# A fused encoder layer on one core: the first sequence's normed operand built from its loaded transposed x, with the row scales spread by four transposes

## The chip, the cores and the metric

One Trainium2 chip, and one of its cores. A core has a matrix engine (PE, with its weight loads shown as PEld), a vector engine (DVE), a scalar engine (ACT), a general engine (POOL) and a queue that issues transfers (SP). The metric is the device time of one execution in microseconds (us), as the median of several runs.

## What is computed

Two sequences of 512 tokens by 1024 features go through the same encoder layer. Cut to what this change bears on:

```python
h = rms_norm(x, ln1)             # x * rsqrt(mean(x*x) + EPS) * ln1, per token
proj = h @ w_in                  # q, k, v, u, g_att, g_ssm
...                              # windowed attention on q, k, v
...                              # state-space branch on u: a recurrence in time, both ways
x = x + mixed @ w_out
h2 = rms_norm(x, ln2)
return x + square(relu(h2 @ w_up)) @ w_down
```

Every product is made in three passes: each float32 operand is cut into a high part (rounded to float32r) and a low part (what the rounding left), and high by high, high by low and low by high are added up. So every operand of a product costs a copy on ACT (high) and a subtraction on DVE or POOL (low).

## The kernel before, in words

Almost all matmuls are 128x128 weights by 512 columns. The normed x stands transposed on chip, as eight blocks k of 128 features by 512 tokens for each sequence, with a high and a low tile: hT[0] for the first sequence (act_104 and act_105 in the order of instructions below), hT[1] for the second (act_106 and act_107).

**The front (lines 351 to 518).** The keys and values of the first sequence are made straight from x_t, its x as the host lays it out already transposed: eight strips k (xr of x_t, wr of the weights) are loaded; split_strip (327) makes high and low of xr times the gain of ln1, in hT[1]'s tiles, and of wr; strip_products (337) adds 12 matmuls for each strip into four banks, the heads. Since the tokens' scales are missing in it, scaled_heads (345) multiplies them in when ACT reads the four banks. Three of these banks are the same three that all later products take in turn (acc, line 81), so the first later product waits until ACT has read the first head.

The normed operand of both sequences is made another way: x is loaded by rows (xs, 128 tokens by 1024 features), square_rows (300) makes each token's mean square on ACT and its power -0.5 on POOL, scale_rows (308) multiplies the rows on DVE, and turn_rows (311) transposes one block k of four row tiles on PE (four transposes), from whose bank ACT takes the high part with the gain and DVE the low part.

**The columns.** Next come 24 columns of the projection (u, g_att, g_ssm), each with 24 matmuls for each sequence (products, 182, line 187 in the profile). They are a generator, and pull(n) emits as many of them as n units are worth, two units a matmul. They fill PE wherever the stage at hand leaves it free. The weights of column i+1 are cut into high and low (split, 169: line 177 on ACT, 178 on DVE) at the fourth and tenth matmul of column i, so where a pull stands decides where these lie on ACT and DVE. Total work is fixed: what is pulled early is missing later. some(n), in the same way, emits n small DVE instructions of the 73 that make the recurrence's coefficients.

**After the front.** pull(140); then the tables (557): 16 rounds, in each of which DVE and ACT prepare a piece (bm, transposed by PE at 610), PE multiplies it (641), and ACT writes the inputs h of the recurrence (646, 647), with pulls between; then 12 small transfers (665 to 667) and pull(28). Then the recurrence (714 to 720): 62 steps of four DVE instructions, each fed by the one before, with pull(15) or pull(14) in each. Then state_rows(0) and (1) (723, on ACT and DVE), pull(90) (738), and 32 rounds q (740) in which PE multiplies the states (750, 753) and pulls an even share of what is left of the columns.

In all these stages each engine's instructions stand in a hand-written order: an instruction that waits holds up all that stand behind it on its engine. (DVE, ACT and SP are ordered by the scheduler in the tables.) SP issues the loads in the order written: strips, rows, and the first column's weights.

## Time and profile before

| | |
|---|---|
| median of 3 runs | 1444.52 us (1444.01 to 1444.83) |
| the profiled execution | 1445.04 us |
| its span | 1443.3 us |
| PE, share of the span | 99% |
| DVE, ACT, POOL | 76%, 53%, 17% |

The profile is of one execution. Each row of its timeline gives a start and a duration in us from the start of the span, the engine, the line, the instruction, and in brackets how long the engine sat idle before it and what ended that. Rows of like instructions may be merged (x3). Instructions of one engine overlap in it: the next may start before the last has landed, so the distance from start to start (the pitch) is what an engine spends, and start plus duration is when others may use the result. A view of waits adds up who waited for whom; the chain is the path followed back from the last instruction.

### The profile page before, as it was taken

To read this page: it belongs to the slowest core of one execution; us is meant where nothing else is said; L and a number is where in the kernel's file an instruction comes from. 1 tells how busy PE (TensorE), PEld (TensorE's weight loads), DVE (VectorE), ACT (ScalarE), POOL (GpSimd) and SP (SyncE) were. 2 spreads that over 40 slices of the span, in tenths; PEclk is the share of its full clock that TensorE was granted. 3 is DMA by queue.
4 is the path that set the end of the run, shared out by engine and by line. 5 is a ranking of instruction groups with operands and counts; after the bars stand their busy time and mean duration, and the time that the engine had idled before them with its cause. 6 is when DMAs were issued, how large, how long until landed. Compare 5 with 4: busy or idle time off the path is not lost.

```text
span 1443.3 us, 22044 instructions
## 1 busy us (share of the span) xinstructions
PE 1435.6 (99%) x7997; PEld 1228.0 (85%) x7997; DVE 1094.9 (76%) x1978; ACT 762.3 (53%) x1359; POOL 244.1 (17%) x396
## 2 busy tenths in 40 slices
PE   9999999999999999999999999999999999999998
PEld 8888888889999999988888888888888888888887
DVE  7999959995458999988976588777776597575644
ACT  7678861224448887894444255455454443333332
POOL 3144443004244432263100000000000000000000
PEclk9999999999999999999999999999999999999999
DMA  7356549529651533345552344444442983464341
GB/s 297 97 170 189 168 147 327 206 91 314 227 180 59 162 107 100 119 140 189 194 190 91 129 136 173 161 160 155 151 143 96 363 319 102 146 201 145 121 131 59
DMA packets 102204, 240.23 MB, mean 166 GB/s; under 512 B 12330, under 2 KB 25130, under 8 KB 102096
## 3 DMA queue, kind: packets, MB, share of 16 engines
q1 hardware_dynamic: 62304, 139.94, 29.9%
q0 software_dynamic: 16320, 48.28, 10.2%
q10 hardware_dynamic: 23472, 50.61, 9.5%
q8 instruction: 63, 1.03, 0.3%
q14 instruction: 45, 0.37, 0.1%
HBM read 169.02 MB, written 81.82 MB: 174 GB/s over the span
## 4 chain that ended last, share of the span: by engine, by line
PE 84%; DVE 8%; issue 4%; DMA 2%; ACT 1%; POOL 1%; DVEq 0%; SPq 0%; ACTq 0%; POOLq 0%
PE bank L118 14%; PE bank L120 14%; PE bank L119 14%; PE acc L187 9%; PE acc L125 6%; PE acc L919 5%; PE po L1002 2%; PE sps L970 2%; PE sps L641 2%; PE tps L986 2%; PE sps L753 2%; PE acc L120 2%; PE acc L119 2%; PE acc L118 2%; DVE t L716 2%
## 5 line engine op out<-in xcount | busy, mean ns | idle before, releaser
L187 PE MATMUL acc<-act,c_hi 128*128 128x512 f32 x768 | 243.7, 395 | 0.0
L119 PE MATMUL bank<-b_lo,a_hi 128*128 128x512 f32 (+1 forms) x449 | 174.4, 389 | 0.0
L120 PE MATMUL bank<-b_hi,a_lo 128*128 128x512 f32 (+1 forms) x449 | 174.4, 389 | 0.0
L118 PE MATMUL bank<-b_hi,a_hi 128*128 128x512 f32 (+1 forms) x449 | 174.4, 389 | 0.0
L187 PEld LDWEIGHTS acc<-act,c_hi 128*128 128x128 f32 x768 | 142.3, 188 | 27.8 <-ACT act L316 0.9
L1714 ACT CAST a_hi<-d_a 128x1024 fp32r<-128x1024 f32 x56 | 59.1, 1055 | 177.4 <-PE bank L119 173.2
L187 PE MATMUL acc<-act,c_lo 128*128 128x512 f32 x384 | 151.3, 394 | 0.0
L1715 DVE TENSOR_TENSOR a_lo<-d_a,a_hi 128x1024 fp32r<-128x1024 f32 x56 | 68.5, 1223 | 98.5 <-ACT a_hi L1714 98.5
L118 PE MATMUL bank<-act,act 128*128 128x512 f32 x368 | 143.2, 389 | 0.0
L119 PE MATMUL bank<-act,act 128*128 128x512 f32 x368 | 143.2, 389 | 0.0
L120 PE MATMUL bank<-act,act 128*128 128x512 f32 x368 | 143.2, 389 | 0.0
L919 PE MATMUL acc<-w_hi,act 128*128 128x256 f32 x512 | 114.0, 291 | 0.1
L119 PEld LDWEIGHTS bank<-b_lo,a_hi 128*128 128x128 f32 x449 | 84.3, 188 | 17.5
L120 PEld LDWEIGHTS bank<-b_hi,a_lo 128*128 128x128 f32 x449 | 84.3, 188 | 17.5
L118 PEld LDWEIGHTS bank<-b_hi,a_hi 128*128 128x128 f32 x449 | 84.3, 188 | 17.3
L919 PEld LDWEIGHTS acc<-w_hi,act 128*128 128x128 f32 x512 | 87.0, 189 | 4.0 <-PE sps L970 0.3
L187 PEld LDWEIGHTS acc<-act,c_lo 128*128 128x128 f32 x384 | 72.2, 188 | 14.7 <-DVE c_lo L178 0.8
L125 PE MATMUL acc<-act,gc_hi 128*128 128x512 f32 x256 | 81.2, 394 | 0.3 <-POOL act L1066 0.3
L118 PEld LDWEIGHTS bank<-act,act 128*128 128x128 f32 x368 | 69.1, 188 | 14.4
L120 PEld LDWEIGHTS bank<-act,act 128*128 128x128 f32 x368 | 69.1, 188 | 14.3
L119 PEld LDWEIGHTS bank<-act,act 128*128 128x128 f32 x368 | 69.1, 188 | 14.2
L980 ACT ACTIVATE p<-p,nmx 128x257 f32<-128x257 f32 (+1 forms) x128 | 72.0, 563 | 16.5 <-DVE nmx L974 15.5
(365 smaller groups left out, 3424.4 us busy)
## 6 DMA issues: line engine op xcount, KB each, us to landing
d_a<-a_scr SPq DMA_DIRECT2D x56, 512.0 KB, 3.6
raws<-in_w_up_dram SPq DMA_DIRECT2D x32, 512.0 KB, 4.0
a_scr<-t ACTq DMA_DIRECT2D x64, 256.0 KB, 3.0
k<-in_w_down_dram SPq DMA_DIRECT2D x32, 512.0 KB, 5.6
c_raw<-in_w_ug_dram SPq DMA_DIRECT2D x48, 256.0 KB, 4.1
ct_scr<-ctab POOLq DMA_DIRECT2D x16, 512.0 KB, 4.8
ctab_in<-ct_scr POOLq DMA_DIRECT2D x16, 512.0 KB, 6.4
a_scr<-a ACTq DMA_DIRECT2D x32, 256.0 KB, 2.0
```

The costliest lines, as they stand in the source:

```text
L118: PE.matmul(ps, a[0], b[0], start=first, stop=False)
L119: PE.matmul(ps, a[0], b[1], start=False, stop=False)
L120: PE.matmul(ps, a[1], b[0], start=False, stop=last)
L125: PE.matmul(ps, w[wi][:, k, :], rows[yi], start=k + p == 0, stop=k == KT - 1 and p == 2)
L187: PE.matmul(ps, w[wi][:, k, :], hT[s][hi][:, k, :], start=n == 0, stop=n == 3 * KT - 1)
L641: PE.matmul(ps[:, i * P:(i + 1) * P], bm[:, ri, g, :], u_sb[:, gp * SH + g, :], start=True, stop=True)
L716: V.tensor_mul(t1, h[:, i], a8r)
L753: PE.matmul(o, ctab[:, g0 % SI + g, ri, 0:T * CH], st[:, ri, g].rearrange("p s k -> p (s k)"), start=False, stop=ri == 1)
L919: PE.matmul(self.ps, hT[sq][act][:, k, col:col + P], w[:, k % 4, :], start=i == 0, stop=i == 3 * KT - 1)
L980: S.activation(p, p, AF.Exp, bias=self.nmx[:, h:h + 1], scale=-1.0, accum_out=self.sums[:, h, self.qb:self.qb + 1])
L1714: S.copy(hi, src)
L1715: V.tensor_sub(lo, src, hi.bitcast(F32))
```

## The change

What it does, in the order of the diff below:

- Row tiles have five buffers in place of eight. The tiles of x_t's strips (xr) have eight, so that all stay; the heads' copies get their own tile kv.
- square_rows, for the first four row tiles, has POOL spread each token's scale over 128 columns (wide).
- spread_scales: four transposes on PE turn that into a bank in which the scales of all 512 tokens stand in every partition. It is placed between strips 4 and 5, in the bank of the warm-up matmuls (idle).
- normed_strip(k): DVE multiplies strip k in place by the gain and by that bank; ACT copies the high part to hT[0]. strip_low(k): DVE (even k) or POOL (odd k) subtracts the low part. They stand among strips 5 to 7 and after.
- The first sequence's scale_rows (four) and turn_rows (eight, with 32 transposes) go.
- The second sequence's squares and scales come after all this, and more columns are pulled ahead of its turn_rows: 24 + 66 units in place of 12 + 54. Since some() has taken fewer coefficients by then (59 of 73 in place of 64), the loop `while some(4): pull(6)` runs four times in place of three. Later pulls are 142 in place of 140, and 64 in place of 90 after the recurrence.

```diff
@@ -287,14 +287,13 @@
         lam_sb = sc.tile([P, 3, GROUPS], F32, name="lam_sb")
         pr, pi = [sc.tile([P, 9, GROUPS], F32, name=n) for n in ("pr", "pi")]
         factors = sc.tile([P, NT], F32, name="factors")
-        xs, scales, turned = [], {}, {}
-        for t in range(NT):
-            xs.append(xin.tile([P, D], F32, tag="xt", name="xt", bufs=NT))
+        xs, scales = [], {}
         rel_sb = xin.tile([N_BUCKETS + 1, N_HEADS], F32, name="rel_sb")
         oh_sb = xin.tile([N_BUCKETS + 1, LINE], F32, name="oh_sb")
         ln_sb = xin.tile([N_HEADS, LINE], F32, name="ln_sb")
 
         def load_rows(t):
+            xs.append(xin.tile([P, D], F32, tag="xt", name="xt", bufs=5))
             SP.dma_start(xs[t], x[t * P:(t + 1) * P, :])
 
         def square_rows(t):
@@ -304,6 +303,10 @@
             scales[t] = factors[:, t:t + 1]
             GP.tensor_scalar_add(ss, ss, EPS)
             GP.tensor_tensor(scales[t], ss, neg_half[:, 0:1], op=ALU.pow)
+            if t < NB:
+                if not t:
+                    spread.append(xin.tile([P, NB, P], F32, name="wide"))
+                GP.tensor_copy(spread[0][:, t], scales[t].to_broadcast([P, P]))
 
         def scale_rows(t):
             V.tensor_scalar_mul(xs[t], xs[t], scales[t])
@@ -317,10 +320,11 @@
             V.scalar_tensor_tensor(hT[s][1][:, k, :], ps, gain_1[:, k:k + 1], h.bitcast(F32),
                                    op0=ALU.mult, op1=ALU.subtract)
 
-        strips, heads = {}, []
+        strips, heads, spread, raws_t = {}, [], [], []
 
         def load_strip(k):
-            strips[k] = [xin.tile([P, HALF], F32, tag=tag, name=tag, bufs=6) for tag in ("xr", "wr")]
+            strips[k] = [xin.tile([P, HALF], F32, tag=tag, name=tag, bufs=n) for tag, n in (("xr", KT), ("wr", 6))]
+            raws_t.append(strips[k][0])
             for tile_, src in zip(strips[k], (x_t, w_kv)):
                 SP.dma_start(tile_, src[k])
 
@@ -342,9 +346,23 @@
                 a, b = ((0, 0), (1, 0), (0, 1))[p]
                 PE.matmul(heads[t], act[a][:, t * P:(t + 1) * P], w[b], start=k + p == 0, stop=k == KT - 1 and p == 2)
 
+        def spread_scales():
+            ps = idle
+            for t in range(NB):
+                PE.transpose(ps[:, t * P:(t + 1) * P], spread[0][:, t], ident)
+            spread[0] = ps
+
+        def normed_strip(k):
+            V.scalar_tensor_tensor(raws_t[k], raws_t[k], gain_1[:, k:k + 1], spread[0], op0=ALU.mult, op1=ALU.mult)
+            S.copy(hT[0][0][:, k, :], raws_t[k])
+
+        def strip_low(k):
+            (GP if k % 2 else V).tensor_tensor(hT[0][1][:, k, :], raws_t[k], hT[0][0][:, k, :].bitcast(F32),
+                                               op=ALU.subtract)
+
         def scaled_heads():
             for t in range(NB):
-                kv = xin.tile([P, 2, N_KV, HD], F32, tag="xr", name="kv", bufs=6)
+                kv = xin.tile([P, 2, N_KV, HD], F32, tag="kv", name="kv", bufs=4)
                 S.activation(kv.rearrange("p a h d -> p (a h d)"), heads[t], AF.Copy, scale=scales[t])
                 GP.dma_start(kv_scr[:, t], kv)
 
@@ -459,49 +477,52 @@
         square_rows(0)
         split_strip(3)
         strip_products(3)
-        scale_rows(0)
-        some(2)
+        some(3)
         square_rows(1)
         split_strip(4)
         strip_products(4)
-        scale_rows(1)
         square_rows(2)
         square_rows(3)
-        some(4)
-        scale_rows(2)
+        some(5)
         split_strip(5)
-        scale_rows(3)
+        spread_scales()
         strip_products(5)
         split_strip(6)
+        normed_strip(0)
         split_strip(7)
         split(0)
+        normed_strip(1)
+        strip_low(0)
+        strip_low(1)
+        strip_products(6)
+        normed_strip(2)
         split(1)
-        some(3)
+        normed_strip(3)
+        strip_low(2)
+        strip_low(3)
         square_rows(4)
-        for k in (0, 1):
-            turn_rows(0, k)
-        strip_products(6)
+        normed_strip(4)
+        normed_strip(5)
+        strip_low(4)
+        strip_low(5)
+        strip_products(7)
+        normed_strip(6)
+        scaled_heads()
+        normed_strip(7)
+        strip_low(6)
+        strip_low(7)
+        split(0)
+        split(1)
         square_rows(5)
         scale_rows(4)
-        some(5)
-        for k in (2, 3, 4):
-            turn_rows(0, k)
+        square_rows(6)
         scale_rows(5)
-        square_rows(6)
-        strip_products(7)
-        scaled_heads()
-        some(4)
-        for k in (5, 6):
-            turn_rows(0, k)
+        square_rows(7)
+        pull(24)
         scale_rows(6)
-        pull(12)
-        turn_rows(0, 7)
-        square_rows(7)
-        split(0)
-        split(1)
         scale_rows(7)
-        some(5)
-        pull(54)
+        some(10)
+        pull(66)
         for k in range(KT):
             turn_rows(1, k)
             pull(6)
@@ -669,7 +690,7 @@
                 pending.insert(0, all_lags)
 
             pending = []
-            pull(140)
+            pull(142)
             for c in range(KT):
                 tables(c)
                 if c == 1:
@@ -735,7 +756,7 @@
                 S.dma_start(y_scr[:, :, ga:ga + SI].rearrange("t c g k -> (t c) (g k)"), y.rearrange("p g k -> p (g k)"))
 
             states = [state_rows(0), state_rows(1)]
-            pull(90)
+            pull(64)
             full = None
             for q in range(GROUPS // SH):
                 g0 = q * SH
```

What this does to the order on the engines shows at three places. First **ACT**, from the cast of the first column's weights (c_hi) or a little before it to the reads of the four heads (kv from the banks acc and head). In the names, act_104 is the high part of hT[0], act_106 that of hT[1], xt a row tile, xr and wr a strip's two halves, wh its weights' high part. Before:

```order
L177 CAST c_hi<-c_raw 128x512 x2
L303 ACTIVATE rn_junk,ss<-xt 128x1024
L316 ACTIVATE act_104<-sps,vec 128x512
L316 ACTIVATE act_104<-tps,vec 128x512
L303 ACTIVATE rn_junk,ss<-xt 128x1024
L316 ACTIVATE act_104<-sps,vec 128x512
L316 ACTIVATE act_104<-tps,vec 128x512
L316 ACTIVATE act_104<-sps,vec 128x512
L303 ACTIVATE rn_junk,ss<-xt 128x1024
L348 ACTIVATE kv<-acc,factors 128x512 x3
L348 ACTIVATE kv<-head,factors 128x512
```

Now, from strip 7's split on:

```order
L357 CAST act_104<-xr 128x512
L336 ACTIVATE act_106<-xr,vec 128x512
L337 CAST wh<-wr 128x512
L177 CAST c_hi<-c_raw 128x512
L357 CAST act_104<-xr 128x512 x2
L177 CAST c_hi<-c_raw 128x512
L357 CAST act_104<-xr 128x512
L302 ACTIVATE rn_junk,ss<-xt 128x1024
L357 CAST act_104<-xr 128x512 x3
L366 ACTIVATE kv<-acc,factors 128x512 x3
L366 ACTIVATE kv<-head,factors 128x512
L357 CAST act_104<-xr 128x512
```

Seven of the eight copies of the normed operand, each fed by a DVE product, stand ahead of the first read of a head; before, it was five reads of transposes, and strip 7's split stood further up.

Second **PE**, in the loop over the second sequence's turn_rows (transposes of xt into the banks sps and tps, at line 314, now 317) with three column matmuls (187) behind each. Before, one block and the start of the next:

```order
L314 MATMUL tps<-ident,xt 128x128 x4
L187 MATMUL acc<-act_104,c_hi 128x512
L187 MATMUL acc<-act_105,c_hi 128x512
L187 MATMUL acc<-act_104,c_lo 128x512
L314 MATMUL sps<-ident,xt 128x128 x4
```

Now, at the first to fourth block:

```order
L317 MATMUL sps<-ident,xt 128x128 x4
L187 MATMUL acc<-act_104,c_hi 128x512
L187 MATMUL acc<-act_105,c_hi 128x512
L187 MATMUL acc<-act_104,c_lo 128x512
L317 MATMUL tps<-ident,xt 128x128 x4
L187 MATMUL acc<-act_106,c_hi 128x512
L187 MATMUL acc<-act_107,c_hi 128x512
L187 MATMUL acc<-act_106,c_lo 128x512
L317 MATMUL sps<-ident,xt 128x128 x4
```

Since more columns have been pulled by then, the matmuls in this loop read the second sequence (act_106, act_107), the operand that the same loop is making; before they read the first.

Third **DVE**, at the end of the recurrence (its four instructions are 716 to 719, now 737 to 740; st is a copy of state_rows; c_lo is the low part of a column's weights). Before:

```order
L716 TENSOR_TENSOR t_3638<-h,a8r 128x256
L717 TENSOR_TENSOR t_3639<-h,a8i 128x256
L718 TENSOR_TENSOR t_3638<-t_3638,h 128x256
L719 TENSOR_TENSOR h<-t_3638,t_3639 128x256
L727 COPY st<-h 64x512 x2
L731 COPY st<-h 64x512
L178 TENSOR_TENSOR c_lo<-c_raw,c_hi 128x512 x2
```

Now:

```order
L178 TENSOR_TENSOR c_lo<-c_raw,c_hi 128x512
L737 TENSOR_TENSOR t_3641<-h,a8r 128x256
L738 TENSOR_TENSOR t_3642<-h,a8i 128x256
L739 TENSOR_TENSOR t_3641<-t_3641,h 128x256
L740 TENSOR_TENSOR h<-t_3641,t_3642 128x256
L748 COPY st<-h 64x512 x2
L752 COPY st<-h 64x512
```

A pair of weight subtractions that stood behind the first states' copies now lies inside the recurrence: it holds 20 of them in place of 18. Counted on PE, 152 column matmuls stand ahead of the tables' first transposes in place of 136, 500 ahead of the last line 641 (now 662) in place of 484, and 1011 ahead of the first round q in place of 1008.

## Prediction

> **What bounds the kernel now.** I read the page first, then PE's waits, then the chain of waits in order of time, then the timeline where the chain leaves PE. The page's engine row:
>
> ```profile
> PE 1435.6 (99%) x7997; PEld 1228.0 (85%) x7997; DVE 1094.9 (76%) x1978; ACT 762.3 (53%) x1359; POOL 244.1 (17%) x396
> ```
>
> Two of PE's waits on other engines, the longest of all and the one for the states (us in total, times, longest):
>
> ```profile
> PE tps L372 <- DVE running L369: 1.1, 1, 1.1
> ...
> PE sps L753 <- DVE st L731: 0.4, 1, 0.4
> ```
>
> PE is busy nearly all the time, but a full PE need not be the bound: the column pulls are there to fill it. The chain in the front and the tables (start, us, what):
>
> ```profile
> 30.13 0.70 PE head L343 x3
> 30.83 0.44 PE tps L314 x4
> ...
> 67.98 0.87 PE tps L610 x8
> ...
> 76.52 5.00 PE acc L187 x22
> ```
>
> Up to the last line 641, at 198, the chain is PE alone: whatever makes PE late or early there moves the start of the recurrence by as much. Then it leaves PE:
>
> ```profile
> 198.47 0.91 PE sps L641 x8
> ...
> 209.91 1.58 DMA lag_scr<-ks
> ...
> 212.10 0.42 DVE t L716
> ...
> 213.69 0.43 DVE t L716
> ...
> 219.93 0.68 DVE c_lo L178
> ```
>
> From 212.10 to 319.4 it is DVE's recurrence, 1.59 us a step (212.10 to 213.69), while PE runs columns. The two meet where the first states are multiplied (timeline; the bracket is idle time before and its releaser):
>
> ```profile
> 319.43 1.10 ACT L729 COPY st<-h 64x512 f32<-64x512 f32 x1 [9.04 <-DVE h L719]
> 320.47 0.38 PE L750 MATMUL sps<-u_sb,toep 128*128 128x128 f32 x2
> 320.68 0.61 PE L753 MATMUL sps<-st,ctab_in 128*128 128x128 f32 x4
> ...
> 328.93 0.71 PE L753 MATMUL sps<-st,ctab_in 128*128 128x128 f32 x4 [0.41 <-DVE st L731]
> ```
>
> The first state lands at 319.43 + 1.10 = 320.53, and PE is there at 320.47. So PE time saved ahead of 320 is worth something only if it makes the recurrence start earlier; behind it, each column matmul already done saves its own time.
>
> **The change, part by part.** Times are against the profiled execution's 1445.04; the median, 1444.52, is 0.52 lower.
>
> *Transposes.* Eight blocks of four, 0.44 each (row 30.83), go and one such group comes: -3.52 + 0.44 = -3.08 of PE.
>
> *Pulls ahead of the tables.* Before 12 + 54 + 8x6 + 3x6 + 140 = 272 units, now 24 + 66 + 8x6 + 4x6 + 142 = 304: 16 matmuls more, at 5.00/22 = 0.227, is +3.64. Without any new wait PE thus comes to the tables 0.56 later, not 3 earlier.
>
> *The read of the heads.* PE needs the first head's bank for the first column, and ACT reads it only behind seven copies of the normed operand, each of which waits for a DVE product. Rows of the timeline for such steps:
>
> ```profile
> 17.66 1.11 POOL L306 TENSOR_TENSOR factors<-ss,neg_half 128x1 f32<-128x1 f32 x1
> ...
> 17.97 0.72 ACT L332 ACTIVATE act<-xr,vec 128x512 fp32r<-128x512 f32 x1
> 18.59 0.60 ACT L333 CAST wh<-wr 128x512 fp32r<-128x512 f32 x1
> 18.86 0.75 DVE L309 TENSOR_SCALAR xt<-xt,factors 128x1024 f32<-128x1024 f32 x1
> 19.12 0.72 ACT L332 ACTIVATE act<-xr,vec 128x512 fp32r<-128x512 f32 x1
> 19.52 0.74 DVE L334 SCALAR_TENSOR_TENSOR act<-xr,vec,act 128x512 fp32r<-128x512 f32 x1
> 20.07 0.86 PE L343 MATMUL acc<-wh,act 128*128 128x512 f32 x3
> 20.18 0.68 DVE L335 TENSOR_TENSOR wl<-wr,wh 128x512 fp32r<-128x512 f32 x1
> 20.78 0.74 DVE L334 SCALAR_TENSOR_TENSOR act<-xr,vec,act 128x512 fp32r<-128x512 f32 x1
> ...
> 22.87 0.60 PE L314 MATMUL sps<-ident,xt 128*128 128x128 f32 x4
> ```
>
> ```profile
> 24.77 1.07 ACT L303 ACTIVATE rn_junk<-xt 128x1024 f32<-128x1024 f32 x1
> ...
> 29.95 1.85 ACT L348 ACTIVATE kv<-acc,factors 128x512 f32<-128x512 f32 x3
> ```
>
> Pitches: ACT 0.62 for a scaled copy, 0.53 for a cast; DVE 0.66 for a scalar-tensor product, 0.60 for a subtraction, landing after 0.74 and 0.68; 0.05 for a hand-over, my allowance. The new product reads one operand from a bank, which no row here shows in this form; I take the 0.66. Now forward from the spread. It takes strip 5's place at 20.07 and lands at 20.67 (0.60, row 22.87). POOL's fourth power ends at 17.66 + 1.11 = 18.77; the last two spreading copies (128 columns each) would have to take 1.2 together to delay PE, and a copy four times as wide takes 0.61 (row L888 below), so they are hidden.
>
> - DVE product 0 at 20.72, landed 21.46. ACT copy 0 at 21.5, then strip 7's two at 22.03 (landed 22.75) and 22.65, the weights' cast at 23.18.
> - DVE strip 7's lows at 22.8 and 23.46, c_lo 24.06, product 1 at 24.66, low 0 at 25.32, product 2 at 25.92.
> - ACT copy 1 at 25.45, copy 2 at 26.7, the second cast at 27.23 (landed 27.83). DVE c_lo at 27.88, product 3 at 28.48 (29.22), low 2, product 4 at 29.74, product 5 at 30.4.
> - ACT copy 3 at 29.27, the fifth row tile's square 29.8 to 30.85, copy 4 (landed 31.45), copy 5. DVE low 4 at 31.5, product 6 at 32.1 (landed 32.84).
> - ACT copy 6 at 32.9, first head at 33.43, read by 34.1 (1.85/3 = 0.62, and 0.7 to land).
>
> PE: strips 5 to 7 take 22.87 - 20.07 = 2.80 each, so it is done at 20.07 + 0.44 + 8.40 = 28.9 and waits until 34.1: +5.2. Bounds: if DVE never waited for ACT, product 6 would land at 20.72 + 6x0.66 + 2x0.63 + 5x0.60 + 0.74 = 29.7 (six products, strip 7's two, five subtractions), the head be read at 31.0, a wait of 2.1; with each of some fifteen steps in the chain 0.1 longer, at its landing instead of its pitch, 6.7.
>
> *The second sequence's loop.* PE's matmuls now read the block that the loop has just made. ACT and DVE there:
>
> ```profile
> 40.89 0.75 DVE L317 SCALAR_TENSOR_TENSOR act<-sps,vec,act 128x512 fp32r<-128x512 f32 x1 [1.73 <-ACT act L316]
> ...
> 41.29 0.69 ACT L316 ACTIVATE act<-tps,vec 128x512 fp32r<-128x512 f32 x1 [0.44 <-PE tps L314]
> ```
>
> ```profile
> 48.06 0.74 DVE L317 SCALAR_TENSOR_TENSOR act<-tps,vec,act 128x512 fp32r<-128x512 f32 x1
> ```
>
> Five blocks in 48.06 - 40.89 = 7.17: DVE, with four small instructions behind each low part, goes at 1.43 a block; PE at 0.44 + 3x0.227 = 1.12. PE comes to the first matmul that reads a low part 0.44 + 0.68 + 0.44 + 0.23 = 1.79 after it began the first transposes; that part is ready after 0.60 + 0.69 + 0.75 and hand-overs, 2.1: a wait of 0.3, then 0.31 more at each of six blocks. (At the last the rel-table matmul of line 515 stands ahead.) Together +2.2; from 1, if DVE gains on it, to 4, if the small ones are all of the slow kind.
>
> *POOL.* The odd low parts, at the price of its like (last columns: busy us, mean ns, idle before):
>
> ```profile
> L1066 POOL TENSOR_TENSOR act<-act,act 128x512 fp32r<-128x512 f32 x16 | 20.4, 1292 | 4.5 <-ACT act L1069 4.4
> ...
> L888 POOL COPY kd<-kn 128x512 f32<-128x512 f32 x8 | 4.9, 610 | 0.0
> ```
>
> The last stands behind the four heads' transfers, ends near 38, and is read by PE 22 matmuls after 34.1, at 39: covered, but by a microsecond only. If the heads came early, this would be late next. SP's row loads wait for ACT's squares of earlier tiles, done long before.
>
> *A pause of PE.* The trace has no pause of 5 us; the nearest is the start:
>
> ```profile
> 1.07 3.78 PE L372 MATMUL tps<-running 128*128 128x128 f32 x16 [1.07 <-DVE running L369]
> ...
> 5.19 1.62 PE L343 MATMUL acc<-wh,act 128*128 128x512 f32 x3 [0.33 <-DVE wh L333]
> ...
> 6.61 0.56 PE L343 MATMUL head<-wh,act 128*128 128x512 f32 x1
> ...
> 7.00 0.86 PE L343 MATMUL acc<-wh,act 128*128 128x512 f32 x3
> ...
> 7.94 0.86 PE L343 MATMUL acc<-wl,act 128*128 128x512 f32 x3
> ```
>
> The first group of four took 1.81 (5.19 to 7.00), the next 0.94: after its idle start PE was at half pace for 5.9 us from its first matmul. If a pause brings that back it costs between 0.9 (those four) and 2.9 (half of 5.9); middle 1.9. The sum takes 0; a rival takes it. The Trainium skill, page TensorE: Matmul & The Clock Gate, section "Part 1: The HAM clock gate", says that an idle window of about 3.4 us drops the clock to half and a busy one lifts it again; an estimate by that page is 1.7 a pause, 3.4 in the sum for two. The start of this trace is of that size; no pause later in it tests the rule.
>
> *The recurrence.* 20 weight subtractions in place of 18. Before, (319.43 - 212.10 - 62x1.59)/18 = 0.49 each: +1.0. PE, with 13 matmuls fewer between line 641 and the first round q (511, 524), would be at the states 2.95 earlier against the recurrence's start, and waits some 4.0 for them: the saved 3 us come to rest here.
>
> *After it.* Three column matmuls fewer are left: -0.68. The pair of subtractions that held the state at 328.93 is done: -0.41, if nothing takes its place.
>
> Sum: -3.08 + 3.64 + 5.2 + 2.2 + 1.0 - 0.68 - 0.41 = +7.9: 1452.9 by the profiled execution, 1452.4 as a median. With the bounds (2.1 to 6.7 and 1 to 4) from 1448.1 to 1455.7.
>
> **The rivals.**
>
> *PE alone is the bound, and it keeps fed.* ACT gets to the heads by 28.9, and the end is not tied to the recurrence: then only the transposes count, 1444.52 - 3.08 = 1441.4. For it: PE's 99%. Against: the states and PE meet within 0.1 us at 320.5. It decides if the first state of the changed kernel is ready when PE comes. Chance 0.05.
>
> *No new wait, but the recurrence holds.* Without the 5.2 and the 2.2: +0.5, 1445.0. For it: between 20 and 33 DVE and ACT are not full (busy times of PE, PEld, DVE, ACT in the stretch):
>
> ```profile
> 20.00:33.00 13.00, 13.00 (x73) 10.86 (x72) 10.30 (x25) 11.01 (x21) 4.58 (x9) 1.00 0.57 224
> ```
>
> Against: the ping-pong above, in which DVE's own work ahead of the head's read, without a wait, already ends after PE's 28.9. Chance 0.10.
>
> *The pauses cost pace.* Two pauses, 5.2 at the heads and 4.0 at the states. Both stretches are followed by work that PE bounds, so 1.9 for one, 3.8 for both: 1454.3 or 1456.2. For it: the start. Against: no other row. Chance 0.30.
>
> **How the numbers follow.** The forecast, 1452.4, has 0.55. About 0.2% (2.9 us) is what a measurement can tell from no change. The forecast and the third rival are slower by more (0.85), the second is within (0.10), the first faster (0.05). The range leaves out these two, 0.15, and the outermost of the rest: from 1447.5, a little below the forecast's lower bound, to 1457.5, a microsecond above the third rival's two pauses.
>
> **What would show it right or wrong.** Right: a PE wait of about 5 us at the first line 187, released by ACT's read of a head; eight short ones after it, released by the second sequence's low parts; the tables' first transposes near 75.9 in place of 67.98; the recurrence about 8 later and 1 longer; a PE wait of about 4 at the first states. Wrong: the first column matmul before 31, or the recurrence starting at 213 or earlier, or first states that wait for PE. Matmuls after the pauses with a pitch of 0.45 would speak for the third rival.

## The result and the profile after

| | before | after |
|---|---|---|
| median | 1444.62 us (1444.01 to 1444.83) | 1462.46 us (1460.39 to 1463.74) |
| the profiled execution | 1445.04 us | 1463.25 us |
| its span | 1443.3 us | 1461.5 us |

The changed kernel is slower: the ratio is 1.0123, with a 95% interval of 1.0105 to 1.0140. The forecast was +7.9 us; measured are +17.8 (medians) and +18.2 (spans). Its direction was right, and the time lies outside its range.

The page's engine row after:

```profile
PE 1438.8 (98%) x7969; PEld 1226.2 (84%) x7969; DVE 1097.1 (75%) x1978; ACT 762.0 (52%) x1359; POOL 252.2 (17%) x404
```

PE's waits on other engines after (us in total, times, longest):

```profile
PE acc L187 <- ACT kv L366: 5.7, 1, 5.7
PE sps L774 <- ACT st L750: 3.3, 1, 3.3
PE acc L187 <- DVE c_lo L178: 2.7, 4, 1.0
PE sps L662 <- DMA u_sb<-u_scr: 1.6, 1, 1.6
PE tps L390 <- DVE running L387: 1.1, 1, 1.1
PE acc L187 <- DVE act L320: 0.8, 4, 0.3
```

Before, no wait but the one at the start was over 0.41. The first row is the predicted pause at the heads, the second the predicted wait for the states. The third and fourth were not predicted. The third lies between 233 and 313, inside the recurrence, at whose end PE waits for the states anyway; the fourth is the load of u_sb, the tables' own copy of the column u. The waits do not show all: PE's busy time rose as well (1438.8 for 1435.6), with 28 instructions fewer. The timeline behind the first pause shows why (later lines are 21 higher than before):

```profile
34.16 1.22 PE L187 MATMUL acc<-act,c_hi 128*128 128x512 f32 x2 [5.67 <-ACT kv L366]
35.18 0.63 PE L187 MATMUL acc<-act,c_lo 128*128 128x512 f32 x1
35.61 1.05 PE L187 MATMUL acc<-act,c_hi 128*128 128x512 f32 x2
...
39.45 0.84 PE L187 MATMUL acc<-act,c_hi 128*128 128x512 f32 x2
40.12 0.40 PE L187 MATMUL acc<-act,c_lo 128*128 128x512 f32 x1
40.36 0.62 PE L187 MATMUL acc<-act,c_hi 128*128 128x512 f32 x2
```

And the same stretch by windows (busy times of PE, PEld, DVE, ACT, POOL, then granted clock, DMA share, GB/s):

```profile
34.16:39.45 5.29, 5.29 (x13) 4.13 (x14) 2.81 (x4) 5.26 (x10) 4.43 (x7) 0.50 0.55 200
39.45:44.75 5.30, 5.30 (x24) 4.35 (x23) 3.23 (x7) 1.31 (x4) 4.85 (x9) 0.96 0.32 99
```

Twelve matmuls took 39.45 - 34.16 = 5.29 in place of 12 x 0.227 = 2.72: after the pause PE ran at half the clock, and that cost 2.57. The further stations (lag_scr is the target of the twelve small transfers):

```profile
211.47 2.02 PE L662 MATMUL sps<-u_sb,bm 128*128 128x128 f32 x16 [1.60 <-DMA u_sb<-u_scr]
...
227.91 0.42 DVE L737 TENSOR_TENSOR t<-h,a8r 128x256 f32<-128x256 f32 x1 [10.33 <-DMA lag_scr<-ks]
...
338.16 0.71 PE L774 MATMUL sps<-st,ctab_in 128*128 128x128 f32 x4 [3.25 <-ACT st L750]
```

From such rows, the starts in both kernels and how the delay grows:

| station | before | after | delay | added |
|---|---|---|---|---|
| tables' first transposes | 67.82 | 78.77 | 10.95 | 10.95 |
| last group of line 641 (662) | 198.31 | 211.47 | 13.16 | 2.21 |
| recurrence, first step | 212.10 | 227.91 | 15.81 | 2.65 |
| recurrence, last step | 317.79 | 335.43 | 17.64 | 1.83 |
| first multiplication of states | 320.68 | 338.16 | 17.48 | -0.16 |
| last multiplication of states | 394.57 | 410.58 | 16.01 | -1.47 |
| end of the span | 1443.3 | 1461.5 | 18.2 | 2.19 |

Forecast were +8.0 at the first row, +1.0 in the fourth, -1.1 in the sixth. Too little were thus the front by 3.0, the way from the tables to the recurrence by 4.9, the recurrence by 0.8, and the tail by 2.2.

### The profile page after: what moved, and what is told of

It reads as the page before. It is cut to its first block, busy times and chain, and to the rows that moved or that the text cites. A ratio compares the mean times of both kernels' runs of the same rounds, so it can differ in the third digit from the quotient of the medians.

```text
span 1461.5 us, 21992 instructions
## 1 busy us (share of the span) xinstructions
PE 1438.8 (98%) x7969; PEld 1226.2 (84%) x7969; DVE 1097.1 (75%) x1978; ACT 762.0 (52%) x1359; POOL 252.2 (17%) x404
## 3 DMA queue, kind: packets, MB, share of 16 engines
q8 instruction: 63, 1.03, 0.3%
## 5 line engine op out<-in xcount | busy, mean ns | idle before, releaser
L187 PE MATMUL acc<-act,c_hi 128*128 128x512 f32 x768 | 246.8, 398 | 6.5 <-ACT kv L366 5.7
L187 PEld LDWEIGHTS acc<-act,c_lo 128*128 128x128 f32 x384 | 72.8, 190 | 18.2 <-DVE c_lo L178 4.4
```

Of the source, the lines that this page charges most:

```text
L187: PE.matmul(ps, w[wi][:, k, :], hT[s][hi][:, k, :], start=n == 0, stop=n == 3 * KT - 1)
```

## Experiments

Two theories stood against each other for the 4.9: the **pull counts** (16 matmuls more ahead of the tables move the columns' own loads against those of the tables), or the **front** (it is late, and all behind it late with it). For the 2.57 the theory was the pause. All times below are medians; the kernel before had 1444.9 to 1445.3 beside them.

**1. Only the pull counts, in the kernel before.**

```diff
-            pull(140)
+            pull(172)
...
-            pull(90)
+            pull(64)
```

> The kernel before, with only the changed pull counts: 172 units ahead of the tables in place of 140 (16 matmuls more), 64 after the recurrence in place of 90. The front stays that of the kernel before, so there is no pause at the heads. Theory 1, the pull counts cause the delays in the tables and at the recurrence's start (the load of u_sb issued late and landing in 6.2 us in place of 3.1, the lag_scr transfers landing 4.8 after their issue in place of 1.6): the tables' first transposes come 3.6 later (71.6 in place of 67.98), and the recurrence's start 3.6 + 2.2 + 2.6 = 8.4 later (220.5), its length is 1.0 to 1.8 longer; time before plus 9, some 1453.5. Theory 2, those delays come from the new front alone (it is late, and its transfers with it): the recurrence starts 3.6 later (215.7), is 1.0 longer, and 0.7 comes back after it: before plus 4, some 1448.5.

Measured: 1451.87, +6.8, ratio 1.0047 (1.0035 to 1.0060). The tables began at 71.53, the last line 641 came at 203.90 (+5.6), the recurrence at 217.86 (+5.8), and it was 1.1 longer. So the load of u_sb is theory 1's, the lag_scr transfers are not its alone. The kernel before, with the issues of u_sb, of the table store and of the next weights (c_raw):

```profile
185.84 8.07 SPq L633 DMA_DIRECT2D u_sb<-u_scr  x2
...
193.31 0.89 POOL L628 DMA_DIRECT2D ct_scr<-ctab  x1 [1.77 <-DVE ctab L627]
198.31 1.95 PE L641 MATMUL sps<-u_sb,bm 128*128 128x128 f32 x16
199.22 1.35 SPq L167 DMA_DIRECT2D c_raw<-in_w_ug_dram  x2
```

The same with the changed pull counts:

```profile
196.44 0.89 POOL L628 DMA_DIRECT2D ct_scr<-ctab  x1 [1.45 <-DVE ctab L627]
196.77 0.35 SPq L167 DMA_DIRECT2D c_raw<-in_w_ug_dram  x1
...
197.21 1.25 SPq L633 DMA_DIRECT2D u_sb<-u_scr  x1
...
198.56 0.91 SPq L167 DMA_DIRECT2D c_raw<-in_w_ug_dram  x1
...
203.90 2.52 PE L641 MATMUL sps<-u_sb,bm 128*128 128x128 f32 x16 [1.98 <-DMA u_sb<-u_scr]
```

Before, the next weights are asked for behind the last line 641; now one of their loads goes out just ahead of that of u_sb, and PE waits. That the one delays the other is read from this order; it was not tried by itself. PE then lost pace twice, each time for 3.41 us from 205.26 and from 328.14. Its timeline at the states:

```profile
327.34 0.71 PE L753 MATMUL sps<-st,ctab_in 128*128 128x128 f32 x4 [2.34 <-ACT st L729]
327.88 0.39 PE L750 MATMUL sps<-u_sb,toep 128*128 128x128 f32 x2
328.11 1.03 PE L753 MATMUL sps<-st,ctab_in 128*128 128x128 f32 x4
328.79 1.20 PE L187 MATMUL acc<-act,c_hi 128*128 128x512 f32 x2
```

Full pace for the first 0.8 behind the pause, then 1.03 for four matmuls that took 0.71 in the first row, and 1.20 for two that take 0.62 at full clock. The loss adds up: 1.98 and 2.34 of waits, 1.7 of pace behind each, less 0.41 of the wait that was there before and 0.68 for three matmuls fewer at the end, is 6.6 of the 6.8.

**2. Only the front: the changed kernel with the pull counts of before.** pull(142) became pull(110), pull(64) became pull(90).

> The changed kernel with the pull counts of before: 110 units ahead of the tables in place of 142 (so that 136 column matmuls stand ahead of their first transposes, as before), 90 after the recurrence in place of 64. The front, with its pause of 5.7 us at the heads and the slow pace behind it, stays. Theory 1 (pull counts): the tables' first transposes come 3.6 earlier than in the changed kernel (75.2), the recurrence starts 8.4 earlier (219.5), and is 0.8 to 1.8 shorter; time some 9 under the changed kernel's 1462.5, about 1453.5. Theory 2 (front): only 3.6 + 1.0 - 0.7 = 4 under it, about 1458.5, with u_sb and lag_scr as late as in the changed kernel.

Measured: 1455.12, +10.1, ratio 1.0067 (1.0053 to 1.0081): 7.3 less than the changed kernel. The tables began at 74.78, u_sb came in time (a wait of 0.3), the recurrence began at 219.91, 13.84 behind the last line 641 (13.79 before, 16.44 in the changed kernel), and took as long as before. The two halves add up: 6.8 + 10.1 = 16.9 of 17.8. The forecast, split the same way, had 3.64 + 1.0 - 0.68 - 0.41 = 3.55 for the pulls and -3.08 + 5.2 + 2.2 = 4.3 for the front.

**3. The pause filled with work.**

```diff
+        (last_hi, _), (last_wh, _) = strips[7]
         strip_products(7)
+        warm = sps()
+        for _ in range(20):
+            PE.matmul(warm, last_hi[:, 0:P], last_wh, start=True, stop=True)
```

> The changed kernel with 20 matmuls more behind strip 7's (of its own operands, into a bank that nobody reads), 20 x 0.227 = 4.5 us of PE work in the pause at the heads; the products are as before. PE still gets the first head's bank at 34.16. If the pause brings the half pace behind it (13 matmuls at 0.43 in place of 0.227), this pace is gone: the first column matmuls go at 0.227 at once, the tables' first transposes come 2.5 earlier (76.3 in place of 78.8), and the time is 2.5 less than the changed kernel's. If the pace comes from something else in that stretch (transfers, weight loads, the new operand), nothing changes but the waits: 78.8 again, and the same time.

Measured: 1458.21, 4.3 less than the changed kernel. PE behind the filled pause:

```profile
34.10 0.73 PE L187 MATMUL acc<-act,c_hi 128*128 128x512 f32 x2 [1.17 <-ACT kv L366]
34.67 0.39 PE L187 MATMUL acc<-act,c_lo 128*128 128x512 f32 x1
34.90 0.62 PE L187 MATMUL acc<-act,c_hi 128*128 128x512 f32 x2
```

Full pace at once: the half pace comes from PE's idleness. The tables began 1.76 earlier, not 2.5, since PE came to the loop sooner and waited for ACT and DVE there (0.66 and 0.28 at its second block); the recurrence 3.8 earlier, since the lag_scr transfers were quicker as well (14.5 from the last line 641 to the first step, 16.4 in the changed kernel). So not all of the 4.3 is the pace.

**4. The first head read early.** strip_products(7) and split(1) move up; one head is read behind the third block, the others behind the eighth.

```diff
         split(0)
+        split(1)
+        square_rows(4)
...
         strip_products(6)
+        strip_products(7)
         normed_strip(2)
-        split(1)
+        scaled_head(0)
         normed_strip(3)
...
```

> The changed kernel with another order in the front: strip 7's products and the first column's second weight split are emitted ahead of the normed operand's third block, ACT reads the first head behind that block's copy (about 27.3 in place of 33.42), the other three heads come behind all eight blocks, and the fifth tile's square stands further up. If ACT's place for this read is what costs the pause and with it the slow pace, both go: the first column matmul at 28.5 to 29.5 in place of 34.16, pace 0.227 from the start, the tables' first transposes 5.2 + 0.5 + 2.5 = 8.2 earlier (70.6). If the delays in the tables and at the recurrence come from the pull counts (theory 1), they stay and the time is 8.2 less than the changed kernel's, 1454.3; if they come from the late front (theory 2), they go too: 8.2 + 4.8 less, 1449.5. If instead DVE's chain of products is the limit (rival to the read's place), PE waits for low parts in the first column and the transposes come at 74 or later.

Measured: 1462.54, no gain, though the pause is gone. PE:

```profile
28.60 0.73 PE L187 MATMUL acc<-act,c_hi 128*128 128x512 f32 x2
...
42.24 0.33 PE L317 MATMUL sps<-ident,xt 128*128 128x128 f32 x1 [0.90 <-DVE xt L312]
...
44.96 0.49 PE L187 MATMUL acc<-act,c_hi 128*128 128x512 f32 x1 [1.26 <-ACT act L319]
...
46.67 1.41 PE L187 MATMUL acc<-act,c_hi 128*128 128x512 f32 x2
```

The first column starts 5.6 earlier, but 14 us on PE waits for what ACT and DVE have not done (the second sequence's scales and copies), and then runs at half pace from 46.78 to 50.20. The tables began at 75.98. So the place of the read made the pause, but moving it alone only moves PE's waits: the work of ACT and DVE that stood ahead of the read now stands ahead of the second sequence's loop. The rival is right in its number (74 or later) and not in its waits: PE waited for low parts in the first column for 0.33 at the longest. Of the time won, 3.4 was still there at the first multiplication of states; behind the wait of 3.26 there the clock was at 0.50 for 6.83 us, and from the first to the last multiplication it took 75.06 in place of 72.42.

**5. One of the two pull counts alone, in the kernel before.** 172 ahead of the tables, 90 kept.

> The kernel before with 172 units in place of 140 ahead of the tables, and the 90 after the recurrence left as they were. In the run with both counts changed (172 and 64: +6.8) PE waited 2.0 for u_sb, ran some 1.6 slower behind that (granted clock 0.96 from 200 to 240), waited 2.3 for the states, and ran some 1.7 slower behind that (0.91 and 0.92 from 320 to 340). Theory A, only PE's own idle time and slow pace count: 13 more matmuls (2.95) fill the wait of 2.3, so this wait and the slow pace behind it go, and the recurrence, which ends as late as before (its last step at 324.6), costs nothing: +3.6, some 1448.6. Theory B, the recurrence's late end is what counts: it stays at +6.8, 1451.9.

Measured: 1449.22, +4.3, ratio 1.0029 (1.0018 to 1.0039). Its waits of PE:

```profile
PE acc L187 <- DVE c_lo L178: 1.9, 2, 1.4
PE sps L641 <- DMA u_sb<-u_scr: 1.8, 1, 1.8
...
PE sps L750 <- ACT ys L760: 0.6, 1, 0.6
...
PE sps L753 <- ACT st L729: 0.3, 1, 0.3
```

The recurrence ended as late as in experiment 1 or later (its last step at 325.52, in place of 324.61), and yet the kernel is 2.6 faster: theory A. The four waits add up to 4.6, less the 0.4 that was there before: 4.2, the loss. The clock did not fall here.

**6. A lead of one block in the second sequence's loop.** pull(66) became pull(60), pull(142) became pull(148).

> The changed kernel with 60 units in place of 66 pulled ahead of the loop over the second sequence's blocks, and 148 in place of 142 behind it: PE multiplies each block one block later than it is transposed, all else as in the changed kernel. If the eight short waits come from the hand-over from PE to ACT to DVE and back (a block that is read as soon as it is made), they go: the tables' first transposes 2.2 earlier (76.6 in place of 78.8), the time 2.2 less. If DVE's own pace in that loop is the limit (a low part and four small instructions, 1.5 to 1.6 a block, against 1.12 of PE), a lead of one block is eaten up within three blocks: 0.3 to 1.0 earlier. The pause at the heads, the slow pace behind it and what follows from the pull counts stay.

Measured: 1461.27. From the first column matmul (34.60) to the tables (79.24) it took 44.64, as in the changed kernel (44.61). In the loop itself, from the first transposes to the matmuls of line 536 behind its last block, it took 10.21 in place of 11.66: the first four blocks went at 1.14 each, the next three at 1.29, 1.26 and 1.72, as DVE ate up the lead. The 1.46 won there was lost behind the loop, where PE took 2.0 longer for the same matmuls, with waits of 0.30 for the last block's low part and 1.11 for a weight's (66.87). So a lead alone gains nothing in the whole, and the DVE rival is nearer; the next experiment tests it.

**7. The same lead, and two small instructions a block.** As 6, with some(2) in the loop in place of some(4).

> The lead of one block once more (60 units ahead of the loop), and with it two small coefficient instructions a block in place of four; the others follow behind the loop, where six units stand to every four of them, so that 124 units in place of 148 follow and 152 matmuls stand ahead of the tables, as in the changed kernel. If DVE's own pace was the limit in the loop (that the lead alone gave nothing, 44.6 from the first column matmul to the tables' first transposes in both, speaks for it), a block now takes DVE 0.66 + 2 x 0.24 = 1.14, about PE's 1.12: the short waits go, and the tables' first transposes come 2.0 to 2.2 sooner after the first column matmul (42.5), if the later coefficients do not hold them. If PE in that loop is slow for another reason (its pace behind the pause), it stays at 44.6.

Measured: 1459.51, and 41.05 for the same stretch, 3.56 less; 0.85 of it is a shorter slow stretch behind the pause (nine matmuls in 3.76, 1.72 lost, in place of 2.57). In the loop it took 9.20, which is also what the kernel before took (9.20): with the lead and less on DVE, the loop's whole loss of 2.46 is gone. The tables began 3.67 earlier than in the changed kernel, and at the recurrence's start 3.3 of that was left; at the last multiplication of states it was gone (410.62 against 410.58). PE at the states here, and then in the changed kernel:

```profile
335.32 1.22 PE L774 MATMUL sps<-st,ctab_in 128*128 128x128 f32 x4 [3.25 <-ACT st L750]
336.34 0.63 PE L771 MATMUL sps<-u_sb,toep 128*128 128x128 f32 x2
```

```profile
338.16 0.71 PE L774 MATMUL sps<-st,ctab_in 128*128 128x128 f32 x4 [3.25 <-ACT st L750]
338.71 0.39 PE L771 MATMUL sps<-u_sb,toep 128*128 128x128 f32 x2
```

The same pause, half pace behind the one, full pace behind the other. From the first to the last multiplication of states it took 75.30 here and 72.42 there, for the same work.

**8. The wait for the states filled.** The changed kernel with pull(90) for pull(64).

> The changed kernel with 90 units after the recurrence, as before, in place of 64; the 142 ahead of the tables stay. PE then has 13 more matmuls (2.95) where it waited 3.25 for the first states. Theory (PE's idle time and slow pace are all that counts): that wait shrinks to 0.3, what slow pace there is behind it in some executions (the stretch from the first to the last multiplication of states took 72.4 in the profiled run of the changed kernel and of the lead alone, 74.0 to 75.3 in others of the same work with the same wait) goes too, and the time is 3 to 4.5 less than the changed kernel's 1462.5: 1458 to 1459.5, with a smaller spread. If the late recurrence itself is what counts, the time stays at 1461 to 1462.5.

Measured: 1458.10, 4.4 less than the changed kernel, as the theory has it. The wait at the states was 0.35, and the last step of the recurrence came at 333.60, only 1.8 earlier. Of the 3.8 between the two profiled executions, 1.3 was there already at the recurrence's start, where the edit has done nothing yet: behind the pause at the heads the clock was at 0.50 for 3.41 us here and for 6.83 there. From there to the last multiplication of states 2.3 came on top, about the 2.9 by which the wait shrank less a new one of 0.65 (line 771, at 341.56).

**9. The front reordered, pull counts as before.** The core of the edit, with strip 7's high parts ahead of the first copy, and split_high and split_low the two halves of split:

```diff
         split_strip(6)
+        strip_high(7)
         normed_strip(0)
         split_strip(7)
...
+        normed_strip(3)
+        scaled_head(0)
         strip_low(2)
...
+        scaled_head(1)
...
+        split_high(0)
         normed_strip(6)
         normed_strip(7)
+        split_high(1)
...
-        some(10)
-        pull(66)
...
+        some(12)
+        pull(60)
...
             turn_rows(1, k)
             pull(6)
-            some(4)
+            some(2)
```

> The changed kernel with its operand (no transposes for the first sequence), but the front's instructions in another order: ACT makes strip 7's high parts ahead of the first copy of the normed operand, both weight splits come early, the first two heads are read between the copies, low part 7 stays on POOL; the second column's weights are split among the last copies, and the later squares and scales stand between small coefficient steps; the second sequence's loop has a lead of two blocks and two small instructions a block in place of four; pull counts so that 136 matmuls stand ahead of the tables, and 90 units after the recurrence, as before. If PE's idle time and pace are all that counts, and the order keeps it fed, only the saved transposes are left: the first column matmul near 28.6, no PE wait over 0.5 in the front, the tables' first transposes at 64.7 to 65.5 (67.8 before), the recurrence's start near 209 (212.1), the time 1441 to 1442. If the recurrence's start hangs on its own transfers or on DVE, it stays near 212, PE waits 3 at the states, and the time is 1444.5 or a little above. If DVE still falls behind in the front, PE waits for low parts and the time lies between 1445 and 1452.

Measured: 1447.50, ratio 1.0017 (1.0008 to 1.0026): 15 less than the changed kernel, and still 2.6 slower than the kernel before. The first column matmul came at 28.01, the tables began at 66.20, 1.6 earlier than before, and the last line 641 came at 198.46, 0.15 later. Between them, PE on its second piece (start, us, idle before), and the windows row from 65 to 80:

```profile
75.59 0.88 PE L662 MATMUL tps<-ident,bpre 128*128 128x128 f32 x6 [0.97 <-DVE bpre L652]
```

```profile
65.00:80.00 15.00, 13.91 (x77) 11.54 (x77) 14.97 (x29) 10.95 (x22) 1.88 (x2) 1.00 0.49 159
```

DVE is busy for 14.97 of 15 us (14.86 before), and PE waits for it.

**10. The same with less on DVE ahead of the tables.** Of three half copies on DVE two to ACT, the sum of the factors to POOL, some(4) for some(12).

> The reordered version (1447.5, where PE reached the tables at 66.20, then waited 1.0 for DVE's second piece, and the last line 641 was back at 198.5 as before) with less on DVE ahead of the tables: two of its three half copies of the tables' factors go to ACT, the sum of them to POOL, and only four small coefficient instructions in place of twelve stand ahead of the second sequence's loop; pull counts so that 136 matmuls still stand ahead of the tables. Theory: DVE is the second bound from 20 to 80 (14 to 15 of 15 us busy in 50 to 80), so that what PE saves cannot be used. Then DVE, relieved of 3 x 0.6 = 1.9, lets the tables begin near 65 with no wait of PE for their second piece, the last line 641 comes 1.5 to 2 earlier (196.7), and the time is 1445.5 to 1446. Rival: the tables are paced from inside (DVE has as much to do there whatever comes before), and nothing changes: 198.5 and 1447.5.

Measured: 1448.44. The theory fails: PE reached the tables at 67.78 - 2.16 = 65.62, and waited.

```profile
67.78 0.44 PE L662 MATMUL tps<-ident,bpre 128*128 128x128 f32 x2 [2.16 <-DVE bpre L652]
```

The last line 641 came at 198.60. The scheduler put other pieces of the tables on DVE ahead of the first one, and one of these (line 671) took 1.85 in place of 0.75, beside POOL's new sum (1.46). Three kernels whose tables began at 66.2, 67.8 and 67.8 had their last line 641 at 198.5, 198.3 and 198.6: what PE gains ahead of the tables it waits for DVE at their start. Whether DVE's work in the tables or what stands ahead of it sets that pace, these runs do not separate.

**11. The reordered front with nine matmuls more ahead of the tables.** pull(128) for pull(110).

> The reordered version (1447.5) with 128 units in place of 110 ahead of the tables: 9 column matmuls, 2.05 us, more. In three runs whose tables began at 65.5 to 67.8 the last line 641 came at 198.3 to 198.6 all the same, with PE waiting for DVE in between; so what PE saves ahead of the tables is not used there. If PE's idle time is all that counts, these 9 fill it (waits of 1.0 and 0.4 in the tables go, and the tables begin at 68.2), the last line 641 comes at 198.5 to 199.2, 9 matmuls fewer are left behind the recurrence, and the time is 1445.5 to 1446.2: about that of the kernel before, no better. Rival: the load of u_sb falls beside those of the next weights, as with 16 matmuls more, PE waits 2 for it, and the time stays at 1447.5 or above.

Measured: 1449.42, not what was expected. The tables began at 69.29, 1.5 later than before, and the last line 641 came at 200.42, 2.1 later; u_sb was not much later (two waits, 0.8 together), so the rival does not hold either. By the last multiplication of states the profiled run was 0.55 behind experiment 9's; the rest arose in the last matmul stages, of whose waits the longest is:

```profile
PE bank L118 <- ACT act L1492: 2.1, 1, 2.1
```

Behind it (844.21) the clock was at 0.50 for 3.41 us from 845.36, some 1.7 of pace; the two make 3.9 of the 4.0 that arose there. Why ACT was late there was not tried. That the tables ended 2.1 later shows PE as the bound again as soon as it comes later than before.

## Why the prediction fell short, step by step

Two steps failed. The sum took 0 for the pace behind a pause of PE: the runs showed 2.57 behind the first pause. And it priced the pulls as PE time alone: in the changed kernel the tables came to wait 1.60 for u_sb, and the recurrence started another 2.65 late behind lag_scr, with moved loads and stores in both places as far as the order in the traces tells. The chain of the front was right in its steps: ACT's read of the first head was forecast at 33.43 and came at 33.42.

- **Transposes, -3.08, and no new bound behind them.** The saving as such was not contradicted: the reordered front reached the tables 1.6 earlier, with waits of 0.31, 0.37 and 0.67 on the way (1.35; together 2.95). But the tables' end did not come earlier with it. The sum took PE as the only bound up to line 641 ("Up to the last line 641, at 198, the chain is PE alone"); experiments 9 and 10 show DVE close beside it.
- **Pulls ahead of the tables, +3.64.** As a delay of the tables right (3.71 alone). As a cost wrong: the work is only moved, and 5 shows that of the delay 3.1 came back behind the states (70.77 for that stretch, 73.89 before) where PE had work. What it did cost are new waits, 6.8 with both counts: u_sb 1.98, the states 2.34, and pace behind both. The step asked what 16 matmuls take, and not which loads move with them: each column carries two loads of weights, and in the traces one of them goes out just ahead of that of u_sb.
- **The read of the heads, +5.2.** Right: 34.16 forecast as 34.1, wait 5.67, as PE was done 0.4 sooner than forecast (28.49 for 28.9).
- **"The sum takes 0" for a pause of PE.** This term was mis-sized: 2.57 behind the first pause in the profiled execution, removed by filling the pause (3). The third rival had 1.9 a pause, with a chance of 0.30. Its mechanism is shown, but its sum, 1454.3 to 1456.2, falls short too.
- **The second sequence's loop, +2.2.** Right in size and cause: the loop took 11.66 in place of 9.20, 2.46 more, and experiment 7 takes all of it away by a lead and less work on DVE, where the lead alone gained nothing in the whole.
- **The recurrence, +1.0.** 1.06 in experiment 1, 1.83 in the changed kernel. Of the 0.77 between them, 0.66 is a wait of DVE at 279.04 for ACT's cast of the next weights, which in turn had waited 3.09 for their load; experiments 5 and 7 have the same wait with 1.23 and 1.01.
- **Its start.** That the transfers of lag_scr would end 2.65 later was in no step. With both pull counts alone it is 14.0 from the last line 641 to the first step, with the front alone 13.8, with both 16.4. In the seven traces with 14.5 to 16.4 the store of a gate column goes out 1.15 to 1.19 ahead of the last of the twelve transfers, in the others (13.8 to 14.0) behind it. That is read from traces and was not tried by itself.
- **The wait at the states, some 4.0.** 3.25 to 3.27 in five kernels.
- **After it, -1.09.** -1.47; but with half pace behind the wait it is up to 2.9 worse, in some executions and not in others. That is the likely source of the changed kernel's spread (3.35 over four runs, 0.82 before).
- **The tail, not forecast, +2.2.** From the last multiplication of states to the end it takes 1048.6 to 1048.7 in the three kernels with the old front that were profiled, and 1049.3 to 1053.9 in the ten with the new operand, whose code there is the same. In the changed kernel 0.9 of the 2.2 arises at 766 to 768 and 0.8 at 1201.6, each time where a matmul of line 119 waits for a low part from DVE. Why these come late with the new operand stays open.

Of the 10.3 that the forecast lacks, 2.57 is thus pace, 2.2 the tables (u_sb 1.60, and a wait of 0.65 for ACT), 2.65 lag_scr, 0.8 the recurrence, 2.2 the tail, less 0.4 behind the states; what is left is mostly the half microsecond by which the pause was longer.

## What to carry to other kernels

When an engine is the bound all along, its work costs nothing by being moved; count instead the waits that the move creates, and look which loads and stores are tied to the moved instructions and what stands on the queues at their new time. A pause of PE can cost more than its length, so a saving that opens one can lose more than it saved. And a saving on the first bound is worth only as much as the second bound is behind it: here PE waited for DVE at the start of the tables, and three microseconds of PE could not be cashed in even with the long pauses taken away.

## What the runs showed of the hardware

The granted clock fell to 0.50, each time for 3.41 or 6.83 us. Behind pauses of 5.0 to 6.0 it did so in all five profiles; behind 3.25 to 3.27 at the states in three of five; behind 1.98 and 2.34 in experiment 1 and 2.15 in experiment 11, but not behind 1.60, 1.85, 2.06 and 2.16 in the changed kernel and experiments 5, 3 and 10. In experiment 1 it began 1.36 and 0.80 after PE was back at work.

What looks like chance is mostly where a pause lies. In each trace the changes of the clock lie whole multiples of 3.41 us apart (in the changed kernel: up at 5.75, down at 33.06, up at 39.88). Laid out in steps of 3.41 on these times, all eleven steps at full clock in which PE was busy for 1.44 us or less were followed by half clock; of those with 1.48 or more only one was (1.86 in experiment 4); the starts and the ends of the kernels are left out. The clock came back after the first step in which PE was busy for 3.35 or more; after steps of 2.75 and less it stayed low. The wait for the states, two steps of the changed kernel (3.25) and then of experiment 4 (3.26); the first number behind the comma is PE's busy time in the step, the third from the end the granted clock:

```profile
333.43:336.84 3.41, 1.48 (x8) 1.09 (x6) 3.34 (x10) 0.00 (x0) 0.00 (x0) 1.00 0.28 91
336.84:340.25 3.41, 2.09 (x14) 1.96 (x15) 3.06 (x5) 2.79 (x4) 0.00 (x0) 1.00 0.27 101
```

```profile
330.09:333.50 3.41, 1.37 (x8) 0.98 (x6) 3.34 (x9) 0.00 (x0) 0.00 (x0) 1.00 0.31 92
333.50:336.92 3.42, 2.20 (x11) 2.20 (x11) 2.91 (x5) 2.91 (x4) 0.00 (x0) 0.50 0.30 116
```

Two like pauses, cut by the steps in different places. This is read from the traces; no run moved a pause by itself to test it.

The Trainium skill, page TensorE: Matmul & The Clock Gate, section "Part 1: The HAM clock gate", tells of a free-running window of some 3.4 us. The steps of 3.41 and the late starts fit it. It has the clock fall after at least one idle window. That does not fit the falls behind 1.98, 2.15 and 2.34, and the cost of the first pause, 2.57, is above the 1.7 estimated from that page.

POOL and DVE slowed each other where both subtracted. In experiment 4, DVE's even low parts, the first alone and the second beside one of POOL's, and then POOL's odd ones:

```profile
28.00 0.69 DVE L360 TENSOR_TENSOR act<-xr,act 128x512 fp32r<-128x512 f32 x1
...
30.04 1.37 DVE L360 TENSOR_TENSOR act<-xr,act 128x512 fp32r<-128x512 f32 x1
```

```profile
26.78 1.30 POOL L360 TENSOR_TENSOR act<-xr,act 128x512 fp32r<-128x512 f32 x1 [0.41 <-ACT act L357]
...
29.52 3.04 POOL L360 TENSOR_TENSOR act<-xr,act 128x512 fp32r<-128x512 f32 x2
```

DVE's took 1.37 in place of 0.69, and POOL's 1.52 each (3.04 for two), 1.30 for the one ahead of them.
